# Three query steps ahead of the small inverse, the value projection copied to SBUF, and chunk, state and local products that alternate between the row halves

## Chip, cores and metric

The kernel runs on 1 core of one Trainium2 chip. The metric is the device time of one execution in microseconds (us); the times shown are medians of repeated runs. TensorE (PE) does the matmuls and transposes, VectorE (DVE), ScalarE (ACT) and GpSimd (POOL) the elementwise work, and SyncE (SP) issues most of the DMAs.

## The reference, cut to what matters

A trunk of two layers over 256 tokens of 1024 channels, all in float32:

```python
for l in range(DEPTH):                       # DEPTH = 2
    proj = x @ w_in[l]
    y_pool = multiscale_pool(proj[..., :256], pool_w[l], pool_scale[l])
    rw_in  = centred_token_shift(proj[..., 256:1216], mu_prev[l], mu_next[l])
    y_rwkv = rwkv7_bidir(rw_in, ...)          # a forward and a backward scan, 4 heads of 64
    y_attn = gqa_axial(proj[..., 1216:], ...) # 8 query heads, 2 key heads of 64, all 256 tokens
    y = concat([y_pool, y_rwkv, y_attn]) @ w_o[l]
    x = layer_norm(ALPHA * x + y)
    x = layer_norm(ALPHA * x + hier_moe(x))   # 32 experts, 2 per token
```

One step of the RWKV scan, per head, with a state of 64x64:

```python
sk    = state @ kk_t
state = state * w_t - outer(sk, kk_t * a_t) + outer(v_t, k_t)
y_t   = state @ r_t
```

The token shift is `f + mu_prev * (f[t-1] - f) + mu_next * (f[t+1] - f)`.

## The kernel before, in words

Each layer is a mixer (`mixer`, L243 to L1011), then the routing (`route_all`), then the experts (`experts`). The expert weights stream through a ring of 22 SBUF slabs of 1 MB, 192 slabs a layer, loaded by SP in the order of the program; a slab's DMA is issued when its slot is free. Slabs of the mixer (weights and work tiles) share this ring, so the first 22 expert slabs of a layer load while its mixer runs.

The scan is computed in four chunks of 64 tokens. Each of the two directions `d` has 4 heads and 4 chunks; a tile of 128 rows holds two heads on its two row halves (`hh`, `half(0)` and `half(1)`), or two chunks by the parity of their number (`par`). The steps of the mixer's own chain, in the order of the program:

- Projections, shifts, the decay's cumulative products, and the operands `ZR`, `Bt`, `Kt` (L552 to L656). `lp` (L658 to L670): products of 32-token blocks.
- `lane_steps` (L688): six DVE steps that invert 16x16 triangular blocks, called one at a time as a generator `lanes`.
- Chunk products (`chunk_prod`, L714, tile `ap`): one call makes 16 matmuls of 64 rows, contracting over one row half, into one PSUM bank, and one masked DVE product that reads it. Four calls, each `d` and `hh`, with a lane step in front of each (L733 to L740). Then `Bn`, two sets of transposes, with the last lane steps; `AT16`, `Tp` and its transposes `TA`, `TB` by DVE (L741 to L757).
- The small inverse: products `i1` to `i5` (L787 to L849) build the inverse of a 64x64 block from 16x16 and 32x32 blocks. ACT makes the eight copies of `TTf` (L820). The value shift `vf` (L797) reads the value projection from its PSUM bank `rv[1]`.
- Key products (L850): `chunk_prod` four times from `Kt`, through the generator `key_prod`. Then `xk`, `psb` and `bon`, `Kn`, and the products `gw`, which give `Gn` and `W2` (L870 to L885).
- State products `nh` and `js` (L893 to L925), one bank for each `d` and `par`; `chain` (tile `st`), and `local_out` (tile `ya`, L944), one bank and one ACT copy for each `par`. Then `yb`, the group norm and the gate.

Beside this chain runs a second one, the generator `side` (L299), whose steps are put into the program by `upto(n)` (L523): it advances `side` until its n-th `yield`. Its steps: 1 to 8 receptance and value projection (banks `rv[0]`, `rv[1]`); 9 to 16 pooling input and key/value projection (banks `pp`, `kv`), ending with the ACT copies `u`; 17 the key normalisation and rotation (`krs`, L378 to L387); 18 to 25 the query steps k = 0 to 7 (two matmuls `pq` of 128x512 each; each also takes one step of `pooling()`, on POOL; k = 3 also transposes the keys); 26 query normalisation and rotation on ACT, DVE and POOL; 27 the pooling product `pl`; 28 and 29 query transposes; 30 the router's bias; from 31 scores, softmax, transposes and value products of the attention, then the product with `w_o`.

The order of instructions on every engine is the order of the program. PSUM has two tags: `bank` (tag r, 5 banks) for the chain and `bankc` (tag c, 3 banks) for most of `side`. `rv[1]` and the two `pq` banks are of tag c. In the program before, `upto` stands so: 15, 15, 15, 16 after the four chunk products; 17 after `i1` and the value shift; 18 after `i2`; 19 ahead of `i5`; one more step after each of the four key products (to 23); `24 + d` after each `xk`; 26 to 29 in `gw`; 31 to 34 in `nh`; 36 to 42 in `js`; 44, 46, 48, 51 around `chain` and `local_out`. So query steps k = 0 and 1 stand inside the inverse, k = 2 to 5 among the key products, k = 6 and 7 behind `xk`.

Of the kernel before, what the change touches and what calls it, by code (L numbers as in the profile page):

```python
# [13 lines left out]
OP = mybir.AluOpType  # L14
# [3 lines left out]
T = 256  # L18
# [50 lines left out]
def tile_encoder(ctx: ExitStack, tc: tile.TileContext, x_tok, x_t, w_a0, w_a1, w_b0, w_b1, w_o,  # L69
# [53 lines left out]
    E, EX, EB = mixer_slabs()  # L123
# [119 lines left out]
    def mixer(l, P, x, E, EX, block, wb, resid):  # L243
# [55 lines left out]
        def side():  # L299
# [77 lines left out]
            Va = cut(E[2], 3840, [128, 2, 128])  # L377
            krs = []  # L378
            tail = [cut(E[2], 512 * n + 320, [128, 128]) for n in range(1, 6)]
            for i in range(2):  # L380
                ps = ps_kv[:, 256 * i:256 * i + 256]
                A.copy(Va[:, i], ps[:, 128:256])
                rk = rms(ps[:, 0:128], 2, "rk", tail[0])
                kr = rope(ps[:, 0:128], 2, gck, gsk, i, tail[1 + i], tail[3 + i])
                G.tensor_tensor(kr, kr, rk.rearrange("p (h d) -> p h d", d=1).to_broadcast([128, 2, 64]), op=OP.mult)
                krs.append(kr)
            yield  # L387
            rq, qrs = [], []
# [408 lines left out]
        for j in range(2):  # L797
            shift(rv[1][:, T * j:T * j + T], vf[:, j], 6 + j)
        upto(17)

        def key_prod(d):
            at = s4(4 + d).rearrange("p (h q a t) -> p h q a t", h=2, q=4, a=2)
            for hh in range(2):
                chunk_prod(Kt[d], d, hh, at)
                yield
            ATk[d] = at.rearrange("p h q a t -> p (h q) a t")

        kp = [key_prod(d) for d in range(2)]
        for d in range(2):
# [4 lines left out]
            TN.append(t_)  # L814
        upto(18)
        for d in range(2):
# [33 lines left out]
        for d in range(2):  # L850
            for _ in kp[d]:
                upto(sent[0] + 1)
            to_tok(lambda j, i: ZR[d][:, 0, j, 128 * i:128 * i + 128], "Zn", ZR[d][:, 0])
        for d in range(2):
# [4 lines left out]
            A.copy(ATb[d][:, :, 0], ps)  # L859
            upto(24 + d)  # L860
        psb = bank("psb")
# [8 lines left out]
        for d in range(2):  # L870
            w2 = s2([128, 8, 64], "W2")
            for h in range(2):
# [16 lines left out]
        for d in range(2):  # L889
            HT.append(ZR[d][:, 1].rearrange("p j (c t) -> p j c t", t=64))  # L890
            IN.append(s1([128, 2, 2, 64], "IN"))
            PJ.append(late[:, 1, d].rearrange("p (j c) t -> p j c t", j=2))
        for d in range(2):  # L893
            for par in range(2):
                nn = 1 if par else 2
                cs = [2 * i + par for i in range(2) if 2 * i + par != order[d][0]]
                p1 = bank("nh").rearrange("p (j c t) -> p j c t", j=2, t=64)
                for c in cs:
                    for jh in range(2):
                        for hh in range(2):  # L900
                            q = 4 * hh + 2 * jh + c // 2
                            mm(p1[half(hh), jh, c // 2], Gn[d][half(par), q], ATb[d][half(par), q, 1])
                            if c == nn:
                                mm(p1[half(hh), jh, 2], Gn[d][half(par), q], nat(Bn[d], q, par))
                for c in cs:
                    V.tensor_tensor(HT[d][:, :, c], HT[d][:, :, c], p1[:, :, c // 2],
                                    op=OP.subtract)
                V.tensor_tensor(IN[d][:, :, par],
                                eye64.rearrange("p (j t) -> p j t", j=1).to_broadcast([128, 2, 64]),
                                p1[:, :, 2], op=OP.subtract)  # L910
                upto(31 + 2 * d + par)
        for d in range(2):
            for par in range(2):
                js = [2 * i + par for i in range(2) if 2 * i + par != order[d][3]]
                p2 = bank("js").rearrange("p (j c t) -> p j c t", j=2, t=64)
                for c in js:
                    for jh in range(2):
                        for hh in range(2):
                            q = 4 * hh + 2 * jh + c // 2
                            acc(p2[half(hh), jh, c // 2], nat(Kn[d], q, par), nat(Vn, q, par), c == js[0] and jh == 0)  # L920
                            acc(p2[half(hh), jh, c // 2], nat(Bn[d], q, par), W2[d][half(par), q])
                for c in js:
                    V.tensor_tensor(PJ[d][:, :, c], p2[:, :, c // 2],
                                    pall[d][:, :, c:c + 1].to_broadcast([128, 2, 64]), op=OP.mult)
                upto(36 + 4 * d + 2 * par)  # L925
        St = [{order[d][1]: PJ[d][:, :, order[d][0]]} for d in range(2)]
# [16 lines left out]

        def local_out(par):  # L944
            p1 = bank("ya").rearrange("p (j i t) -> p j i t", j=2, t=64)
            for d in range(2):
                for jh in range(2):
                    for i in range(2):
                        for hh in range(2):
                            q = 4 * hh + 2 * jh + i  # L950
                            acc(p1[half(hh), jh, i], nat(Vn, q, par), ATk[d][half(par), q, 1], d == jh == i == 0)
                            acc(p1[half(hh), jh, i], W2[d][half(par), q], ATb[d][half(par), q, 1])
            A.copy(wkv.rearrange("p j (i r) t -> p j i r t", r=2)[:, :, :, par], p1[:, :, 0:2])

        chain(1)
        upto(44)
# [3 lines left out]
        upto(48)  # L960
        local_out(1)
        upto(51)
        p3 = bank("yb").rearrange("p (j c t) -> p j c t", j=2, t=64)
# [619 lines left out]
```

## Time and profile before

| | |
|---|---|
| median of 3 runs | 1303.68 us (1299.08 to 1311.31) |
| profiled execution | 1308.36 us, its span 1306.6 us |
| granted TensorE clock, mean of the span | 0.870 |
| PE busy | 999.7 us (77%), 7547 matmuls |
| PE weight loads (PEld) busy | 490.5 us (38%) |
| DVE, ACT, POOL busy | 343.0 us (26%), 238.6 us (18%), 98.0 us (7%) |
| DMA | 438.65 MB, 336 GB/s on the mean |

The layers follow each other in the span: mixer of layer 0 to about 193 us, its experts to about 650 us, mixer of layer 1 to about 841 us, its experts to the end. In rows that list instructions, `64*64 64x128 f32` behind an operation is the tile of PE that it uses (rows and columns) and the shape of the output. Matmuls of one group are joined in a row with their count; in float32 one matmul runs as two passes, and the count `x` counts passes. "idle before <-" names what ended the engine's idle time.

### The profile page before, as it was taken

The page shows a single profiled execution, that of the slowest core. Times are in us where ns is not written, and L with a number is a line of the kernel's source. Part 1 is how long each engine was busy: PE and PEld are TensorE (multiplying, and loading weights), DVE is VectorE, ACT ScalarE, POOL GpSimd, SP SyncE. Part 2 cuts the span into 40 slices and gives each one's busy share as a digit, 9 for nine tenths or more (in the row PEclk, how much of TensorE's full clock was granted, in tenths as well). Part 3 has the DMA queues.
Part 4 walks back from the last instruction along what each step waited for, and adds up shares of the span by engine and source line. Part 5 has one row for each costly group of instructions (what it writes and reads, how often), then busy time and mean ns, then how long its engine had stood idle before and what let it go on. Part 6 is the DMA issues. An engine that isn't in the chain of part 4 may idle for free. (4 is left out here: it accounts for less than half of the span.)

```text
span 1306.6 us, 17970 instructions
## 1 busy us (share of the span) xinstructions
PE 999.7 (77%) x7547; PEld 490.5 (38%) x7547; DVE 343.0 (26%) x779; ACT 238.6 (18%) x551; POOL 98.0 (7%) x140
## 2 busy tenths in 40 slices
PE   8798988950997777686697979889429978777754
PEld 7655773330441222120286557732204412222100
DVE  5835653110010000010268286521100100010103
ACT  5224512100110101010251354220001101010100
POOL 1142100000000000000111452000000000000002
PEclk9988998985999988887798999889759997888776
DMA  9302598998999999999940136899989999999994
GB/s 373 153 34 98 214 367 351 419 418 356 401 418 419 420 420 419 419 420 421 417 184 9 35 130 259 325 413 418 419 335 420 419 419 420 420 419 419 420 420 167
DMA packets 63450, 438.65 MB, mean 336 GB/s; under 512 B 7040, under 2 KB 7296, under 8 KB 11520
## 3 DMA queue, kind: packets, MB, share of 16 engines
q1 hardware_dynamic: 62784, 436.61, 81.4%
q8 instruction: 63, 1.03, 0.3%
q10 hardware_dynamic: 576, 0.79, 0.2%
q14 instruction: 27, 0.22, 0.0%
HBM read 436.32 MB, written 1.05 MB: 335 GB/s over the span
## 5 line engine op out<-in xcount | busy, mean ns | idle before, releaser
L172 PE MATMUL pg<-w,xg 128*32 128x512 f32 x1024 | 145.7, 668 | 120.4 <-ACT xg L1205 79.3
L172 PE MATMUL py<-w,hT 128*32 128x512 f32 x1024 | 146.3, 696 | 56.2 <-DMA w<-in_e_w_dram 45.1
L172 PE MATMUL pu<-w,xg 128*32 128x512 f32 x1024 | 157.5, 702 | 41.2 <-DMA w<-in_e_w_dram 40.8
L1236 DVE TENSOR_TENSOR h<-h,pu 128x512 f32<-128x512 f32 x16 | 11.0, 688 | 435.7 <-PE pu L172 226.6
L1205 ACT ACTIVATE xg<-xg,lnc 128x128 f32<-128x128 f32 x120 | 44.9, 457 | 354.0 <-PE xg L168 246.2
L172 PEld LDWEIGHTS pg<-w,xg 128*32 128x32 f32 x1024 | 25.7, 117 | 221.3 <-ACT xg L1205 82.3
L1266 DVE TENSOR_TENSOR xr<-xr,pc 128x512 f32<-128x512 f32 x56 | 38.5, 687 | 241.0 <-PE pc L172 241.0
L172 PEld LDWEIGHTS py<-w,hT 128*32 128x32 f32 x1024 | 28.5, 116 | 156.2 <-DMA w<-in_e_w_dram 87.9
L168 PEld LDWEIGHTS xg<-OH,x 128*128 128x128 f32 x256 | 64.8, 331 | 53.5 <-issue 52.0
L168 PEld LDWEIGHTS xg<-OH,xr 128*128 128x128 f32 x256 | 64.8, 331 | 53.0 <-issue 51.5
L168 PE MATMUL xg<-OH,x 128*128 128x128 f32 x256 | 75.1, 431 | 5.4 <-PEq L1278 4.1
L168 PE MATMUL xg<-OH,xr 128*128 128x128 f32 x256 | 75.2, 432 | 5.2 <-PEq L1278 3.8
L172 PE MATMUL pc<-y,OHT 128*128 128x512 f32 x128 | 73.9, 674 | 0.0
L1258 ACT COPY y<-py 128x512 f32<-128x512 f32 x32 | 18.7, 585 | 241.5 <-PE py L172 241.5
L231 POOL TENSOR_TENSOR w<-w 128x512 fp32r<-128x512 f32 (+1 forms) x20 | 25.2, 1266 | 499.4 <-ACT w L230 496.9
L172 PEld LDWEIGHTS pu<-w,xg 128*32 128x32 f32 x1024 | 23.9, 116 | 99.4 <-DMA w<-in_e_w_dram 80.3
L269 PE MATMUL wo<-w 128*128 128x512 f32 x192 | 48.7, 409 | 5.3 <-DVE x L514 2.0
L196 POOL TENSOR_TENSOR lnmv<-lnmv,eps 128x1 f32<-128x1 f32 x8 | 4.9, 613 | 537.5 <-PE pc L172 463.5
L269 PEld LDWEIGHTS wo<-w 128*128 128x128 f32 x192 | 36.6, 194 | 16.5 <-DVE x L514 2.4
L172 PEld LDWEIGHTS pc<-y,OHT 128*128 128x128 f32 x128 | 21.4, 201 | 54.9 <-issue 49.2
L230 ACT CAST w<-w 128x512 fp32r<-128x512 f32 (+1 forms) x64 | 37.3, 602 | 22.2 <-PE wo L269 13.8
L168 PE MATMUL pq<-w 128*128 128x512 f32 x64 | 35.8, 681 | 0.5 <-DVE w L283 0.5
(330 smaller groups left out, 1095.4 us busy)
## 6 DMA issues: line engine op xcount, KB each, us to landing
w<-in_e_w_dram SPq DMA_DIRECT2D x384, 1024.0 KB, 19.9
w<-in_w_b_dram SPq DMA_DIRECT2D x8, 1024.0 KB, 18.7
w<-in_w_o_dram SPq DMA_DIRECT2D x8, 1024.0 KB, 20.0
w<-in_w_a_dram SPq DMA_DIRECT2D x4, 1024.0 KB, 13.4
lnr<-in_ln_rows_dram SPq DMA_DIRECT2D x12, 256.0 KB, 12.8
w<-in_w_a_dram SPq DMA_DIRECT2D x4, 448.0 KB, 6.4
w<-in_w_a_dram SPq DMA_DIRECT2D x2, 896.0 KB, 12.4
w<-in_cols_dram SPq DMA_DIRECT2D x2, 790.0 KB, 10.4
```

What stands on the lines that cost most here:

```text
L168: PE.matmul(ps, lhsT=lhsT, rhs=rhs, start=start, stop=True, skip_group_check=True)
L172: PE.matmul(ps, lhsT=lhsT, rhs=rhs, start=start, stop=stop)
L196: G.tensor_tensor(mv[:, 3:4], mv[:, 2:3], eps[:, 4:5], op=OP.pow)
L230: A.copy(hi, src)
L231: (V, G)[LOW[m]].tensor_tensor(lo, src, hi.bitcast(F32), op=OP.subtract)
L269: PE.matmul(ps, lhsT=l_[a], rhs=r_[b], start=first and n == 0, stop=last, skip_group_check=True)
L1205: A.activation(t_[:, k], ps[:, k], AF.Identity, scale=lnc["g1"][:, m:m + 1], bias=lnc["b1"][:, m:m + 1])
L1236: V.tensor_mul(h_, h_, ps_u)
L1258: A.copy(y_, py)
L1266: V.tensor_add(o_, o_, ps)
```

## The change

In `side`, the key normalisation moves from ahead of query step 0 to ahead of query step 4; `pooling()` begins at k = 3 instead of 0, its rest and the key transposes come at k = 6 instead of k = 3. Three query steps (k = 0 to 2) are called, by `upto(19)`, ahead of `AT16`, behind the `Bn` transposes; the rest follow at `upto(20)`, `(21)`, `(22)`, `24 + d`, and the query normalisation, step 26, stands behind `xk`.

The value projection is copied by ACT from its bank `rv[1]` to SBUF (`vraw`), behind the `lp` products, and the value shift reads the copy.

`chunk_prod` makes both row halves `hh` in one call: two banks, and matmuls that alternate between them; each of its two masked products is followed by a lane step. `nh`, `js` and `local_out` open two banks, one for each `par`, and alternate their matmuls between the parities; `local_out` is now called per direction `d`, and both its ACT copies stand behind the second call. The number of matmuls and their operands is the same.

```diff
@@ side
-            krs = []
...
-            yield
             rq, qrs = [], []
...
             for k in range(8):
-                next(pool_ops, None)
+                if k == 4:
+                    krs = []
...
+                    yield
+                if k > 2:
+                    next(pool_ops, None)
                 w = wb[1](k)
                 for i in range(2):
                     acc(ps_q[i], xw(k, 128 * i, 128 * i + 128), w, k == 0)
-                if k == 3:
+                if k == 6:
+                    for _ in pool_ops:
+                        pass
                     pkt = bankc("pkt")
@@ behind the lp products
+        vraw = cut(E[1], 2560, [128, 2, T])
+        A.copy(vraw.rearrange("p j t -> p (j t)"), rv[1])
@@
-        def chunk_prod(src, d, hh, at):
-            ps = bank("ap").rearrange("p (q t) -> p q t", q=4)
+        def chunk_prod(src, d, at):
+            ps = [bank("ap").rearrange("p (q t) -> p q t", q=4) for _ in range(2)]
             for q in range(4):
                 jh, i = q // 2, q % 2
                 for par in range(2):
                     t0 = 128 * i + 64 * par
-                    mm(ps[half(par), q].rearrange("p (a t) -> p a t", a=2), src[half(hh), jh, t0:t0 + 64],
-                       ZR[d][half(hh), :, jh, t0:t0 + 64])
-            V.tensor_tensor(at[:, hh].rearrange("p q a t -> p q (a t)"), ps, mb[d], op=OP.mult)
+                    for hh in range(2):
+                        mm(ps[hh][half(par), q].rearrange("p (a t) -> p a t", a=2), src[half(hh), jh, t0:t0 + 64],
+                           ZR[d][half(hh), :, jh, t0:t0 + 64])
+            for hh in range(2):
+                V.tensor_tensor(at[:, hh].rearrange("p q a t -> p q (a t)"), ps[hh], mb[d], op=OP.mult)
+                next(lanes, None)
@@
-            for hh in range(2):
+            if d == 0:
                 next(lanes, None)
-                chunk_prod(Bt[d], d, hh, at)
-                upto(15 + (d + hh) // 2)
+            chunk_prod(Bt[d], d, at)
+            upto(15 + d)
@@ behind the Bn transposes
-            next(lanes, None)
+        upto(19)
+        for _ in lanes:
+            pass
@@ the inverse
-            shift(rv[1][:, T * j:T * j + T], vf[:, j], 6 + j)
-        upto(17)
+            shift(vraw[:, j], vf[:, j], 6 + j)
+        upto(20)
...
-        upto(18)
+        upto(21)
...
-        upto(19)
+        upto(22)
...
-            for _ in kp[d]:
-                upto(sent[0] + 1)
+            key_prod(d)
+            upto(24 + d)
...
-            upto(24 + d)
+        upto(26)
...
-                upto(26 + 2 * d + h)
+                upto(27 + 2 * d + h)
@@ nh; js and its upto(36 + 4 * d + 2 * par), now upto(38 + 4 * d), are changed in the same way
+            p1 = [bank("nh").rearrange("p (j c t) -> p j c t", j=2, t=64) for _ in range(2)]
+            for n in range(2):
+                for jh in range(2):
+                    for hh in range(2):
+                        for par in range(2):
+                            if n < len(cs[par]):
+                                c = cs[par][n]
+                                q = 4 * hh + 2 * jh + c // 2
+                                mm(p1[par][half(hh), jh, c // 2], Gn[d][half(par), q], ATb[d][half(par), q, 1])
...
-                upto(31 + 2 * d + par)
+            upto(32 + 2 * d)
@@
-        def local_out(par):
-            p1 = bank("ya").rearrange("p (j i t) -> p j i t", j=2, t=64)
...
+        def local_out(d):
+            for jh in range(2):
+                for i in range(2):
+                    for hh in range(2):
+                        q = 4 * hh + 2 * jh + i
+                        for m in range(2):
+                            for par in range(2):
+                                acc(pya[par][half(hh), jh, i], W2[d][half(par), q] if m else nat(Vn, q, par),
+                                    (ATb if m else ATk)[d][half(par), q, 1], d == jh == i == m == 0)
+        pya = [bank("ya").rearrange("p (j i t) -> p j i t", j=2, t=64) for _ in range(2)]
...
         local_out(1)
+        for par in range(2):
+            A.copy(wkv.rearrange("p j (i r) t -> p j i r t", r=2)[:, :, :, par], pya[par][:, :, 0:2])
```

## Rows read from the trace of the kernel before

**Rows 1.** Stretches of the span; the first line names the columns, PEclk is the granted clock.
```profile
core 0: us, PE busy (x) PEld busy (x) DVE busy (x) ACT busy (x) POOL busy (x), PEclk, DMA share, GB/s
58.85:64.90 6.05, 0.00 (x0) 0.00 (x0) 5.79 (x9) 1.03 (x3) 0.00 (x0) 0.79 0.48 173
62.33:72.57 10.24, 6.48 (x193) 5.90 (x194) 6.38 (x13) 0.63 (x3) 0.00 (x0) 0.50 0.01 2
64.90:83.72 18.82, 15.85 (x460) 10.93 (x460) 8.56 (x23) 5.96 (x19) 8.59 (x13) 0.71 0.01 3
104.27:118.16 13.89, 10.65 (x99) 8.26 (x99) 6.97 (x18) 6.01 (x16) 4.04 (x5) 0.71 0.55 217
118.16:150.40 32.24, 29.95 (x467) 20.69 (x467) 24.07 (x67) 19.22 (x53) 10.31 (x8) 0.97 0.16 55
193.20:199.70 6.50, 5.89 (x32) 4.67 (x35) 1.71 (x6) 1.50 (x4) 0.00 (x0) 0.74 0.08 30
199.70:323.80 124.10, 72.17 (x469) 30.57 (x461) 18.25 (x44) 11.54 (x25) 0.00 (x0) 0.81 0.98 406
713.00:731.60 18.60, 15.85 (x460) 11.11 (x460) 8.61 (x24) 5.97 (x19) 8.35 (x12) 0.69 0.01 3
752.20:763.30 11.10, 7.41 (x100) 5.93 (x100) 6.98 (x18) 5.93 (x16) 4.06 (x5) 1.00 0.70 275
763.30:796.70 33.40, 29.43 (x467) 20.43 (x465) 27.66 (x67) 19.22 (x53) 20.15 (x16) 1.00 0.13 38
840.80:847.90 7.10, 6.49 (x36) 5.09 (x39) 1.96 (x9) 1.51 (x5) 0.00 (x0) 0.76 0.15 56
```

**Rows 2.** DVE in order of time, 55 to 65 us: start us, us, instruction.
```profile
55.09 0.69 DVE L722 TENSOR_TENSOR w<-ap,kc 128x512 f32<-128x512 f32 x1 [0.90 <-PE ap L172]
...
63.81 1.04 DVE L754 STREAM_TRANSPOSE TA<-Tp 128x512 f32<-128x512 f32 x1
```

**Rows 3.** PE in order of time, 51 to 57 us, the chunk products.
```profile
51.00 1.09 PE L172 MATMUL ap<-w,sga 64*64 64x128 f32 x16
...
53.95 2.09 PE L172 MATMUL ap<-w,sga 64*64 64x128 f32 x48
```

**Rows 4.** PE in order of time, 64 to 88 us, inverse and key products.
```profile
64.91 1.92 PE L172 MATMUL i<-TA,AT 64*64 64x32 f32 x32 [6.07 <-DVE TA L754]
...
76.45 0.85 PE L174 MATMUL i<-TN,w 32*32 32x32 f32 x48
...
78.76 0.44 PE L174 MATMUL i<-TN,w 32*32 32x32 f32 x16 [1.45 <-issue]
79.13 3.56 PE L168 MATMUL pq<-w 128*128 128x512 f32 x4
...
84.75 1.98 PE L168 MATMUL pq<-w 128*128 128x512 f32 x4
86.66 1.09 PE L172 MATMUL ap<-w,sga 64*64 64x128 f32 x16
```

**Rows 5.** ACT in order of time, 57 to 80 us.
```profile
57.14 0.65 ACT L329 COPY w<-pp 128x256 f32<-128x256 f32 x2 [11.85 <-PE pp L168]
...
72.31 0.26 ACT L382 COPY w<-kv 128x128 f32<-128x128 f32 x1
...
75.48 3.00 ACT L820 COPY late<-i 32x256 f32<-32x256 f32 x8
78.50 0.58 ACT L730 COPY Vn<-tk 128x512 f32<-128x512 f32 x1
```

**Rows 6.** PE in order of time, 103 to 120 us, the pooling product.
```profile
109.18 0.65 PE L172 MATMUL pl<-w 64*64 64x256 f32 x4 [2.51 <-DVE w L360]
```

**Rows 7.** Groups of PE, 668 to 800 us: passes | busy us, mean ns | idle.
```profile
L168 PE MATMUL ya<-w,Vn 64*64 64x64 f32 x64 | 4.0, 222 | 0.0
...
L168 PE MATMUL js<-Vn,Kn 64*64 64x64 f32 x48 | 3.4, 230 | 0.0
...
L172 PE MATMUL nh<-w,late 64*64 64x64 f32 x48 | 3.0, 230 | 0.0
```

**Rows 8.** PE in order of time, 44 to 50 us, the lp products.
```profile
44.04 0.76 PE L174 MATMUL lp<-sga,w 64*32 64x32 f32 x64
```

More of the change, by code (lines that the diff above doesn't have):

```diff
@@ L377, in side @@
             Va = cut(E[2], 3840, [128, 2, 128])
-            krs = []
[L379 to L386, printed above, removed]
-            yield
             rq, qrs = [], []
@@ L398, in side @@
             for k in range(8):
-                next(pool_ops, None)
+                if k == 4:
+                    krs = []
+                    tail = [cut(E[2], 512 * n + 320, [128, 128]) for n in range(1, 6)]
+                    for i in range(2):
+                        ps = ps_kv[:, 256 * i:256 * i + 256]
+                        A.copy(Va[:, i], ps[:, 128:256])
+                        rk = rms(ps[:, 0:128], 2, "rk", tail[0])
+                        kr = rope(ps[:, 0:128], 2, gck, gsk, i, tail[1 + i], tail[3 + i])
+                        G.tensor_tensor(kr, kr, rk.rearrange("p (h d) -> p h d", d=1).to_broadcast([128, 2, 64]), op=OP.mult)
+                        krs.append(kr)
+                    yield
+                if k > 2:
+                    next(pool_ops, None)
                 w = wb[1](k)
@@ L797, in mixer @@
         for j in range(2):
-            shift(rv[1][:, T * j:T * j + T], vf[:, j], 6 + j)
-        upto(17)
+            shift(vraw[:, j], vf[:, j], 6 + j)
+        upto(20)
         def key_prod(d):
             at = s4(4 + d).rearrange("p (h q a t) -> p h q a t", h=2, q=4, a=2)
-            for hh in range(2):
-                chunk_prod(Kt[d], d, hh, at)
-                yield
+            chunk_prod(Kt[d], d, at)
             ATk[d] = at.rearrange("p h q a t -> p (h q) a t")
-        kp = [key_prod(d) for d in range(2)]
         for d in range(2):
@@ L893, in mixer @@
         for d in range(2):
-            for par in range(2):
[L895 to L906, printed above, removed]
+            p1 = [bank("nh").rearrange("p (j c t) -> p j c t", j=2, t=64) for _ in range(2)]
+            cs = [[2 * i + par for i in range(2) if 2 * i + par != order[d][0]] for par in range(2)]
+            for n in range(2):
[6 more added lines that the diff above has]
+                                mm(p1[par][half(hh), jh, c // 2], Gn[d][half(par), q], ATb[d][half(par), q, 1])
+                                if c == (1 if par else 2):
+                                    mm(p1[par][half(hh), jh, 2], Gn[d][half(par), q], nat(Bn[d], q, par))
+            for par in range(2):
+                for c in cs[par]:
+                    V.tensor_tensor(HT[d][:, :, c], HT[d][:, :, c], p1[par][:, :, c // 2],
                                     op=OP.subtract)
@@ L909, in mixer @@
                                 eye64.rearrange("p (j t) -> p j t", j=1).to_broadcast([128, 2, 64]),
-                                p1[:, :, 2], op=OP.subtract)
-                upto(31 + 2 * d + par)
+                                p1[par][:, :, 2], op=OP.subtract)
+            upto(32 + 2 * d)
         for d in range(2):
-            for par in range(2):
[L914 to L923, printed above, removed]
+            p2 = [bank("js").rearrange("p (j c t) -> p j c t", j=2, t=64) for _ in range(2)]
+            js = [[2 * i + par for i in range(2) if 2 * i + par != order[d][3]] for par in range(2)]
+            for n in range(2):
+                for jh in range(2):
+                    for hh in range(2):
+                        for m in range(2):
+                            for par in range(2):
+                                if n < len(js[par]):
+                                    c = js[par][n]
+                                    q = 4 * hh + 2 * jh + c // 2
+                                    acc(p2[par][half(hh), jh, c // 2], nat((Kn, Bn)[m][d], q, par),
+                                        W2[d][half(par), q] if m else nat(Vn, q, par), n == jh == m == 0)
+            for par in range(2):
+                for c in js[par]:
+                    V.tensor_tensor(PJ[d][:, :, c], p2[par][:, :, c // 2],
                                     pall[d][:, :, c:c + 1].to_broadcast([128, 2, 64]), op=OP.mult)
-                upto(36 + 4 * d + 2 * par)
+            upto(38 + 4 * d)
         St = [{order[d][1]: PJ[d][:, :, order[d][0]]} for d in range(2)]
@@ L942, in mixer @@
         wkv = s2([128, 2, 4, 64], "wkv")
-        def local_out(par):
-            p1 = bank("ya").rearrange("p (j i t) -> p j i t", j=2, t=64)
[L946 to L953, printed above, removed]
+        def local_out(d):
+            for jh in range(2):
+                for i in range(2):
+                    for hh in range(2):
+                        q = 4 * hh + 2 * jh + i
+                        for m in range(2):
+                            for par in range(2):
+                                acc(pya[par][half(hh), jh, i], W2[d][half(par), q] if m else nat(Vn, q, par),
+                                    (ATb if m else ATk)[d][half(par), q, 1], d == jh == i == m == 0)
+        pya = [bank("ya").rearrange("p (j i t) -> p j i t", j=2, t=64) for _ in range(2)]
         chain(1)
@@ L961, in mixer @@
         local_out(1)
+        for par in range(2):
+            A.copy(wkv.rearrange("p j (i r) t -> p j i r t", r=2)[:, :, :, par], pya[par][:, :, 0:2])
         upto(51)
```

## The prediction

> **What bounds the kernel now.** I read the stretches of the span first (busy time, granted clock and DMA share in each), then the order of time on PE, VectorE (DVE) and ScalarE (ACT) inside a mixer. In the expert stages DMA is the bound: from 199.7 to 323.8 us its share is 0.98 at 406 GB/s while PE is busy 72 of 124 us [rows 1]. In the mixers it is not: shares of 0.01 to 0.16, PE nearly always busy [rows 1]. Just before each expert stage DMA is idle for 6.50 and 7.10 us (share 0.08 and 0.15) [rows 1]: all 22 ring slots are full, and the stream goes on only when the experts free the first slot. So whatever a mixer saves before that point moves the whole rest of the program forward, one for one, once per layer.
>
> Inside a mixer the reader is to see three things. PE stands still for 6.05 us while DVE computes the small inverse: its first inverse product waits 6.07 us for the transpose of Tp, which ends at 64.85 us [rows 1, 2, 4]. The granted clock then falls to 0.50 (1.2 GHz) and stays there from 62.33 to 72.57 us, with the small inverse products that follow [rows 1]. And matmuls of 64 rows run only two at a time: 16 passes of a chunk product take 1.09 us, but 48 passes in a row, of groups on both row halves, take 2.09 us [rows 3].
>
> All sums below are made against the profiled execution: 1308.36 us, of which 1306.6 is the span and 1.8 lies around it. The median of the three runs, 1303.68, is 4.68 lower; I take that off at the end.
>
> **The change part by part,** in us saved per layer.
>
> *Three query steps ahead.* A query step is two matmuls of 128x512 (4 passes); from the start of one to that of the product behind it is 86.66 - 84.75 = 1.91 [rows 4]. Three are 5.73, and they now stand in the hole. The four chunk products there take 1.02 + 2.02 today; as two alternating pairs they should take 2 x 1.02, so PE comes to the hole 1.0 earlier, at 57.85, and is done at 63.6. DVE's chain in front of the transpose of Tp loses one wait, 0.90 for a chunk product of the second row half [rows 2]; I take 0.85. The first inverse product then starts at 64.05, with PE idle 0.5 instead of 6.07. Saved: 5.73 of steps that need no time later, and 0.85. Both ends: if nothing goes ahead, 0; more than the hole, 6.05 + 0.85, cannot be had here.
>
> *Value projection copied out.* The query steps need PSUM banks that the value projection holds until its token shift, which now comes after the steps. One copy of 128x512 on ACT per layer is added; a like one (Vn) took 0.58 [rows 5]. It falls where ACT is idle for 11.85 [rows 5]; cost 0, and 0.6 if that cover were gone. Behind it on ACT wait the copies u, at 57.14, 6 us later. The shift reads SBUF instead of PSUM: 0, with a tenth either way. The moved key normalisation, pooling and key transposes add no instruction and no DMA; POOL keeps their order, and no SP wait changes place.
>
> *The inverse, first product to first key product:* 18.82 and 18.60 [rows 1]. It holds two query steps before and after. At the low clock one of them takes 3.56 instead of 1.98 [rows 4], the earlier one is about 1.0 late, and the two first products take 1.92 each [rows 4], about half of that at full clock: 4.5 lost to the clock. Against it stands a new order on ACT: the key normalisation (72.31 to 75.48, DVE in between) moves from before the second inverse product to after it, in front of the eight copies of TTf, 3.00 us [rows 5]. Counted from the first inverse product these end at 13.6 today; by the same durations they end at 12.8 afterwards, so the stretch can't be shorter than about 13.9. Ends: 4.9 saved if the clock stays up, 0 if it falls all the same: some 4 us of small products still follow one another. Their clock row [rows 1] shows that such work did not raise it. I take 2.8.
>
> *Key products.* Four groups of 1.03 (83.72 to 84.75 [rows 4]) become two: 1.8 saved after switching. Ends: 0 (no overlap) and 2.06.
>
> *The stretch from W2/G products to the first scores,* 13.89 and 11.10 [rows 1]. The query normalisation (step 26) now starts before psb and the Kn transposes instead of after the first of these products. The pooling product waits 2.51 for it today [rows 6]; with 2.7 us more of PE work in between I leave 1.0. But bon and W2 queue on DVE behind the query rotation, and PE's third product group behind bon's bank: half a microsecond goes back. Saved 0.9 in layer 1. In layer 0 the same work ran at a clock of 0.71 against 1.00 [rows 1], worth 2.8; I count 2.0 of it, so 2.9. Ends: 2 us lost (bon and W2 wait for the whole rotation) and 4.5 saved in layer 0, 2 in layer 1.
>
> *nh, js and ya products.* 80, 96 and 128 passes (48 + 32, 48 + 48 and 64 + 64, two interleaved groups each, of which one row stands) busy for 3.0, 3.4 and 4.0 [rows 7], some 31 to 37 ns a pass with two in flight; four in flight would halve them, 5.2 off PE. PE isn't alone there: DVE is busy 24.07 of 32.24, in layer 1 27.66 of 33.40 [rows 1], and the attention steps wait for it. I take 2.2 and 1.2; ends 0 and 5.2. The two ACT copies of wkv, now behind the last product, lie beside the yb products: 0.
>
> One rule speaks against this term. The Trainium skill, "TensorE: Matmul & The Clock Gate", section "Wait — 56ns, not 53.3ns?", says that matmuls never start closer than about 25 ns, however few their columns. Here 64 passes in four row and column strips took 0.76 us, 12 ns each [rows 8], so the row does not bear it out; by the rule the three products would keep 25 ns a pass (saving 2.8 on PE instead of 5.2), and the sum would be some 1.7 us higher.
>
> Sum: layer 0 5.73 + 0.85 + 2.8 + 1.8 + 2.9 + 2.2 = 16.3; layer 1 5.73 + 0.85 + 2.8 + 1.8 + 0.9 + 1.2 = 13.3; together 29.6. 1308.36 - 29.6 = 1278.8, and less 4.7: **1274 us**. The case's own range: with the better end of the inverse and 4.5/2.0 and 4.0/2.5 for the last two stretches 39.6 saved, 1264; with these three at zero 16.8 saved, 1287.
>
> **The rivals.**
> - *Alternation gives nothing*: two in flight stay two, because the second row half's passes queue. The key, nh, js and ya terms and some 0.6 of the first go: 2 x 1.8 + 3.4 + 1.2 = 8.2, 1282. For it: one group alone never has more than two passes in flight. Against it: the 48 passes, 2.09 us instead of 3 x 1.02 [rows 3].
> - *The waits only move*: the inverse stays at the low clock and behind the ACT copies, and bon and W2 eat what the pooling product gains: 2 x 2.8 + 3.8 = 9.4 less, 1283. For it: the two chains on ACT and DVE are as long as before [rows 5]. Against it: the 6 us hole in front of the drop is gone.
> - *DMA hides it*: the first 22 slabs come no earlier, so that only the idle 6.50 + 7.10 [rows 1] can be won: 1290. Against it: the slots of these slabs are freed by the mixer itself and move with it.
> - *The steps do not run ahead*, held by a bank: 11.5 and the clock's 5.6 go, 1291. Against it: both banks are released before the hole.
> - *Slower than before*: PE outruns its instruction supply. It stood 1.45 us in the middle of a product without waiting for anything that the profile shows, after 48 passes in 0.85 us [rows 4]. Ten product groups per layer (4 chunk, 2 each of nh, js, ya) would be issued twice as fast; if each stood 2 us, 40 us are lost: 1314. It decides from 29.6 / 20 = 1.5 us a group. Against it: the 48 overlapping passes ran without a hole [rows 3].
>
> **How the numbers follow.** Forecast 0.60; alternation without effect 0.13; waits that only move 0.15; DMA 0.05; steps not ahead 0.03; slower 0.04. The forecast's range with the next two lies between 1264 and 1287; for the unknown ends on both sides I give 1262 to 1291, which leaves out the slower case, half of the DMA and bank cases, and a tail below. About 1% (13 us) is what a measurement of this kernel can tell from no change. Faster by more than that (under 1290.6): nearly all of the first three and half of the DMA case, 0.89. Slower (over 1316.7): 0.02. Within: 0.09.
>
> **What would show it.** Right, if in the profile after: twelve pq passes stand behind the Bn transposes and the wait of the first inverse product is under 1.5 us; the chunk product groups show 32 passes in about 1.1 us and ya 64 in about 1.1; no stretch of clock 0.50 begins at the inverse, or one of 3.4 us; the key products begin about 15 to 16.5 us after the first inverse product; DMA still pauses some 6 us before each expert stage, about 16 and 30 us earlier than now. Wrong, if the passes per group stay at 55 and 31 ns (alternation), if a new wait of over 2 us stands before i5, gw or ptp (waits move), if the pause before the experts is gone (DMA), or if PE shows gaps by "issue" in the product groups (instruction supply).

## The result, and the profile after

The changed kernel takes 1287.75 us, median of 4 runs (1285.02 to 1289.5), against 1304.68 us (1299.08 to 1311.31) in the same runs of the kernel before: ratio 0.9854, 95% interval 0.9824 to 0.9884. It is 16.9 us faster; 29.6 had been forecast, to 1274. The profiled execution has a span of 1283.1 us, 23.5 under that of before.

The stretches of the span after, the eight that answer to [rows 1] (window, length, busy time of each engine with its instructions, granted clock, DMA share, GB/s):

```profile
core 0: us, PE busy (x) PEld busy (x) DVE busy (x) ACT busy (x) POOL busy (x), PEclk, DMA share, GB/s
65.49:84.60 19.11, 15.63 (x460) 10.21 (x461) 8.70 (x23) 5.09 (x16) 6.83 (x10) 0.73 0.16 57
698.07:719.71 21.64, 16.05 (x461) 10.54 (x461) 8.69 (x23) 5.07 (x16) 6.44 (x9) 0.76 0.15 51
97.25:106.95 9.70, 7.88 (x123) 5.96 (x122) 7.07 (x19) 5.66 (x15) 4.06 (x5) 1.00 0.54 210
732.35:742.06 9.71, 7.89 (x124) 5.97 (x123) 7.08 (x19) 5.66 (x15) 4.06 (x5) 1.00 0.57 212
106.95:135.06 28.11, 24.31 (x445) 16.36 (x444) 22.94 (x67) 18.85 (x53) 10.31 (x8) 1.00 0.19 63
742.06:773.70 31.64, 25.75 (x445) 17.64 (x444) 25.05 (x67) 18.95 (x53) 20.20 (x16) 0.95 0.11 37
179.91:186.77 6.86, 6.86 (x36) 4.52 (x40) 2.39 (x13) 2.87 (x11) 0.00 (x0) 0.57 0.01 1
821.00:825.78 4.78, 4.78 (x30) 2.75 (x33) 1.95 (x11) 2.40 (x11) 0.00 (x0) 0.67 0.00 0
```

Each line has its fellow in [rows 1]. Two of the mixer's parts became shorter here: the gw stretch from 13.89 and 11.10 to 9.7, the one behind it from 32.24 and 33.40 to 28.1 and 31.6. DMA still pauses ahead of the experts (last two lines), so the mixer's gain passes on. The inverse, first product to first key product, did not become shorter: 18.82 and 18.60 before, 19.11 and 21.64 after.

PE in order of time after, chunk products to first inverse product of layer 0 (before: [rows 3, 4]):

```profile
52.69 1.10 PE L172 MATMUL ap<-w,sga 64*64 64x128 f32 x32
...
55.65 1.10 PE L172 MATMUL ap<-w,sga 64*64 64x128 f32 x32
...
59.39 5.32 PE L168 MATMUL pq<-w 128*128 128x512 f32 x12
65.49 1.12 PE L172 MATMUL i<-TA,AT 64*64 64x32 f32 x32 [0.79 <-DVE TA L765]
```

32 chunk passes (16 matmuls of two passes each, made by one `chunk_prod`; before, one made 8) take the time of 16, the twelve query passes fill the hole, and the first inverse product waits 0.79 us instead of 6.07 and takes 1.12 instead of 1.92. So far all is as forecast. The same engine, layer 1, inside the inverse:

```profile
701.57 3.51 PE L168 MATMUL pq<-w 128*128 128x512 f32 x4
705.01 0.75 PE L174 MATMUL i<-IX,TB 32*32 32x32 f32 x64
...
706.28 0.58 PE L174 MATMUL i<-TB,IX 32*32 32x32 f32 x46
711.00 0.29 PE L174 MATMUL i<-TB,IX 32*32 32x32 f32 x13 [4.13 <-issue]
...
714.48 0.79 PE L174 MATMUL i<-TN,w 32*32 32x32 f32 x21 [0.24 <-issue]
715.20 3.52 PE L168 MATMUL pq<-w 128*128 128x512 f32 x4
```

PE stands 4.13 us in the middle of i3, for nothing that its row names (in layer 0 1.49, and 0.78 in i4), and both query steps run at the low clock. Before, the only such stop was in i4, 1.45 us in layer 0 [rows 4] and 1.28 in layer 1. SP's queue after shows what is new beside it:

```profile
705.11 0.33 SPq L1042 DMA_DIRECT2D w<-in_e_w_dram  x1
```

Query step 3 was the last reader of the first half of its weights. Their slab is free when that step ends, now ahead of i2, and SP issues an expert slab of 1 MB into it. What DMA moves while PE stands, in two windows of the changed kernel, 705.00 to 708.50 us and 708.50 to 711.00 us:

```profile
q1 hardware_dynamic: 96, 0.79, 67.9%
...
q1 hardware_dynamic: 48, 0.26, 26.5%
q8 instruction: 1, 0.02, 2.2%
```

(Queue, packets, MB, share of 16 engines.) A packet of the instruction queue comes only in the second window, at 708.61, when most of the slab has passed, and PE goes on 2.4 us after it. That PE lacks instructions is read from this order: in all stops of over 0.2 us in the inverse, in the fourteen traces of this case, PE goes on 2.2 to 2.8 us after a packet of that queue has begun (once 3.4).

In layer 0 the slab is issued ahead of i2 as well, and yet the stop is short:

```profile
71.81 0.33 SPq L1042 DMA_DIRECT2D w<-in_e_w_dram  x1
75.37 0.36 PE L174 MATMUL i<-TB,IX 32*32 32x32 f32 x21 [1.49 <-issue]
```

There the instruction packet began at 72.77, together with the slab's first packet (72.76); in layer 1 it began 2.5 us behind it.

Groups of PE by line and shape after, layer 1, which answer to [rows 7]:

```profile
L172 PE MATMUL ap<-w,sga 64*64 64x128 f32 x128 | 4.4, 275 | 0.0
...
L168 PE MATMUL ya<-w,Vn 64*64 64x64 f32 x64 | 2.2, 226 | 0.0
...
L172 PE MATMUL nh<-w,late 64*64 64x64 f32 x48 | 2.0, 232 | 0.0
```

ya went from 4.0 to 2.2 us, nh from 3.0 to 2.0, and ap, four groups of 32, from 7.5 to 4.4. js gained less here, 3.4 to 2.7; in layer 0, at full clock, it takes 2.2.

### The profile page after: what moved, and what is told of

The parts are those of the page before. It is cut to its first block, busy times and chain, and to the rows that moved or that the text cites. A ratio compares the mean times of both kernels' runs of the same rounds, so it can differ in the third digit from the quotient of the medians.

```text
span 1283.1 us, 17982 instructions
## 1 busy us (share of the span) xinstructions
PE 989.3 (77%) x7547; PEld 478.2 (37%) x7547; DVE 339.4 (26%) x779; ACT 238.8 (19%) x553; POOL 98.2 (8%) x140
## 3 DMA queue, kind: packets, MB, share of 16 engines
HBM read 436.32 MB, written 1.05 MB: 341 GB/s over the span
## 5 line engine op out<-in xcount | busy, mean ns | idle before, releaser
L172 PE MATMUL pg<-w,xg 128*32 128x512 f32 x1024 | 152.2, 695 | 119.9 <-ACT xg L1221 78.8
L172 PE MATMUL pu<-w,xg 128*32 128x512 f32 x1024 | 158.2, 705 | 36.5 <-DMA w<-in_e_w_dram 36.4
L172 PEld LDWEIGHTS py<-w,hT 128*32 128x32 f32 x1024 | 29.6, 118 | 153.9 <-DMA w<-in_e_w_dram 79.7
L230 ACT CAST w<-w 128x512 fp32r<-128x512 f32 (+1 forms) x64 | 37.3, 602 | 22.4 <-PE wo L269 14.0
## 6 DMA issues: line engine op xcount, KB each, us to landing
w<-in_w_b_dram SPq DMA_DIRECT2D x8, 1024.0 KB, 18.7
```

What stands on the lines that cost most here:

```text
L172: PE.matmul(ps, lhsT=lhsT, rhs=rhs, start=start, stop=stop)
L230: A.copy(hi, src)
```

## The experiments

Times are medians of six runs (twelve for the copy of the kernel before), each beside runs of the kernel before on the same chip, whose medians lay between 1304.6 and 1306.5. The two medians of the changed kernel lie 2.1 us apart, so small differences are read from stretches of the traces.

**The kernels again.** No edit. First the kernel before.

> The kernel before, a second time, to see which of its stretches repeat. Theory (the low clock in the stretch from psb to the first scores of layer 0, 10.2 us long, was chance, and the sum counted it as a gain although the median holds it only in part): that stretch comes out near 12.9 us in both layers instead of 15.72 and 12.90; PE's wait of 1.3 to 1.5 us in i4 and the 6.07 us hole repeat; the stretch from the first inverse product to the first key product stays between 16.5 and 19. Rival (the 15.72 us belong to layer 0): 15.5 to 16 again in layer 0.

Median 1308.14 (1298.22 to 1318.38; ratio to the other copies 1.001, 0.9978 to 1.0041). The profiled run has a span of 1296.6, ten less than that of the same program before. psb to first scores (the gw stretch of [rows 1] with psb and the Kn transposes), in both layers, first of the first execution, then of this second one:

```profile
102.45:118.16 15.71, 12.47 (x109) 9.38 (x108) 7.66 (x19) 6.34 (x16) 4.04 (x5) 0.74 0.55 201
750.39:763.29 12.90, 9.21 (x110) 7.05 (x109) 7.67 (x19) 6.25 (x16) 4.06 (x5) 1.00 0.65 244
```

```profile
100.31:113.49 13.18, 10.67 (x109) 8.16 (x108) 7.67 (x19) 6.37 (x16) 4.06 (x5) 0.87 0.62 239
741.95:755.17 13.22, 10.71 (x110) 8.20 (x109) 7.67 (x19) 6.37 (x16) 4.06 (x5) 0.87 0.64 239
```

So the 15.7 us of layer 0 did not repeat, as the theory has it: the clock was lower there in the first execution (0.74 for 0.87). The hole (6.05, 6.06) and the stop in i4 (0.83, 1.05, a little shorter) repeat; the inverse took 16.57 and 16.82.

> The changed kernel itself, a second time, to see what of its trace repeats. Theory (the stall in the small products is made by the slab's transfer and by fast passes in a row): PE's wait in i2 and i3 by nothing that the profile shows is again 3.5 to 5 us in layer 1 and 1 to 2.5 in layer 0; the low clock falls at other places, so that a stretch without a change moves by up to 4 us; median 1286 to 1290. Rival (the 4.13 us were chance): the wait in layer 1 comes out under 2.5.

Median 1289.84, 14.8 us under the kernel before beside it (ratio 0.9871, 0.9829 to 0.9913). The stop in i3 of layer 1 is 3.67 us, 1.85 in layer 0: it belongs to the kernel. The inverse took 17.09 and 23.24.

**The slab later.**

```diff
-            for k in range(8):
+            for k, kw in enumerate((0, 1, 2, 4, 5, 3, 6, 7)):
-                w = wb[1](k)
+                w = wb[1](kw)
-                    acc(ps_q[i], xw(k, 128 * i, 128 * i + 128), w, k == 0)
+                    acc(ps_q[i], xw(kw, 128 * i, 128 * i + 128), w, k == 0)
```

> The changed kernel, with the query steps taking the eight weight blocks in the order 0, 1, 2, 4, 5, 3, 6, 7, so that the first weight slab is freed among the key products and not ahead of the small products i2 and i3; nothing else differs. Theory (the 1 MB expert slab that SP now issues at 71.81 and 705.11 us runs across the fetch of PE's instructions): the stall in i2 and i3 of layer 1 falls from 4.13 us to about 1.5, that of layer 0 stays near 1.5, the stretch from the first inverse product to the first key product goes from 21.6 to about 19.0 us in layer 1 and stays at 19.1 in layer 0; the time is about 2.6 us under the changed kernel's 1287.75. Rival (256 fast passes in a row outrun the supply whatever else DMA does): 4.13 and 21.6 us stay, and so does the time.

Median 1288.59. PE in this version, layer 1, i2 to i4:

```profile
706.36 0.75 PE L174 MATMUL i<-IX,TB 32*32 32x32 f32 x64
...
710.09 0.30 PE L174 MATMUL i<-TB,IX 32*32 32x32 f32 x13 [1.94 <-issue]
...
713.58 0.79 PE L174 MATMUL i<-TN,w 32*32 32x32 f32 x21 [1.27 <-issue]
```

With the slab gone the stop comes after the same passes but lasts 1.94 instead of 4.13. In the DMA queues of this version, from 706.30 to 708.80 us, nothing but the instruction packet is there:

```profile
q8 instruction: 1, 0.02, 2.9%
```

So about 2 us are the transfer's in layer 1 (4.13 and 3.67 in the changed kernel's two executions), and about 1.9 are there without it. In layer 0 nothing was gained: its stops are 2.11 and 1.59 with the slab gone, longer than the 1.5 expected and than the changed kernel's 1.49 and 0.78; there the packet had not come behind the slab. The stretch went to 20.25, not 19.0: a second stop of 1.27, where the changed kernel has 0.24, came in i4. The time is a miss: no gain, though the stretch became shorter; the low clock took some of it back among the key products (12.34 us there in layer 1, 10.72 in layer 0).

**A query step between i2 and i3.**

```diff
-                if k == 4:
+                if k == 5:
                     krs = []
-        upto(20)
+        upto(19)
...
-        upto(21)
+        upto(20)
...
-        upto(22)
+        upto(21)
```

> The changed kernel, with query step 3 between i2 and i3 instead of behind i1, step 4 ahead of i5, and the key normalisation, which has no PE work, behind i5 instead of between i2 and i3. Theory (a stall comes after some 170 fast passes in a row): no stall in i2 or i3; one of about 1.5 us in i4, as in the kernel before, and longer in layer 1 if the slab's transfer falls on it; stretch from the first inverse product to the first key product about 17.5 us in layer 0 and 17.5 to 20 in layer 1, so 1.5 to 5 us under the changed kernel. Rival (the clock alone sets this stretch, and it falls whenever the small products come): 19 us in both layers, time as the changed kernel's.

Median 1286.8, 1.0 to 3.0 under the changed kernel's two medians. The inverse takes 16.16 us in layer 0, with one stop of 0.91, better than expected, and 20.65 in layer 1. PE there:

```profile
706.15 0.81 PE L174 MATMUL i<-TN,w 32*32 32x32 f32 x45
710.56 0.63 PE L174 MATMUL i<-TN,w 32*32 32x32 f32 x19 [3.60 <-issue]
```

No stop in i2 or i3; in layer 1 the slab, issued at 704.42, now falls on i4. Both edits together:

> The changed kernel with query step 3 between i2 and i3, step 4 ahead of i5 and the key normalisation behind i5, and also the weight blocks in the order 0, 1, 2, 4, 5, 3, 6, 7, so that the slab's transfer comes among the key products. Theory: the 3.6 us stall that the step between i2 and i3 alone left in layer 1, beside the slab's transfer, goes to 0.9 as in layer 0; stretch from the first inverse product to the first key product about 16 to 17 us in both layers, the time 3 to 5 us under the version with the step between alone (1286.8), 1282 to 1284. Rival (the stall there isn't the slab's): 20 us in layer 1 and 1287.

Median 1282.91, as expected, 6.9 under the changed kernel on the same chip; the inverse took 16.11 and 15.04 us, its stops in i4 1.32 and 1.16 (and 0.22 in i3 of layer 0):

```profile
707.12 0.50 PE L174 MATMUL i<-TN,w 32*32 32x32 f32 x19 [1.16 <-issue]
```

So both parts are shown by edits: the stop in i3 goes with the step between, and what the slab adds in layer 1 with its own edit (3.60 to 1.16). A stop of 1.2 to 1.3 us in i4 stays with both edits.

**TB in a place of its own.**

```diff
-        TB = s2([128, 16, 2, 16], "TB")
+        TB = cut(E[1], 0, [128, 16, 2, 16])
```

> The changed kernel with TB in SBUF space of its own, so that its transpose on DVE needn't wait until the first i1 group has read AT16. Theory (the holes in front of the small products cost PE time): TB ends 1.2 us earlier, the hole of 1.2 us between the two i1 groups goes, the stretch from the first inverse product to the first key product is 1.1 us shorter in both layers, the time 2 us under the changed kernel's. Rival (PE's supply of instructions sets this stretch): the stall in i2 and i3 grows by what the hole gave, stretch and time stay.

Median 1285.51. The hole between the i1 groups is gone. In layer 0 the rival holds: the stop grew to 3.65 (1.49 and 1.85 in the changed kernel) and the stretch is 19.21 (19.11 and 17.09). In layer 1 it doesn't: the stop is 4.13 (4.13 and 3.67) and the stretch became shorter, 20.67 (21.64 and 23.24), as the theory has it. The time is 4.3 under the changed kernel on the same chip, more than the expected 2; that stays unexplained, as the profiled execution, the slowest of the six, has the span of the changed kernel's (1285.3). With the other two edits:

> The version with step 3 between i2 and i3 and the later slab, with TB in space of its own as well. Theory (the parts add): stretch from the first inverse product to the first key product about 15 us in both layers, time 1280 to 1282. Rival (supply of instructions or the clock take back what the hole gave): as without TB's place, 1283 or more.

Median 1277.93, ratio to before 0.9776 (0.9733 to 0.9819), better than expected; the inverse took 13.25 and 14.50. PE in layer 1:

```profile
694.32 1.12 PE L172 MATMUL i<-TA,AT 64*64 64x32 f32 x32 [1.03 <-DVE TA L765]
695.32 1.12 PE L172 MATMUL i<-w,AT 64*64 64x32 f32 x32
...
703.80 0.56 PE L174 MATMUL i<-TN,w 32*32 32x32 f32 x19 [1.06 <-issue]
```

By the medians TB's place is worth 5.0 us here and was worth 4.3 in the changed kernel, so it pays with the long stop and without it. The inverse is 2.9 and 0.5 shorter than without it, in layer 0 at a higher clock as well (1.00 for 0.89); where the rest comes from isn't shown.

**Four steps ahead,** TB in its place, plain order of the weights.

```diff
-                if k == 4:
+                if k == 6:
                     krs = []
...
-                if k == 6:
+                if k == 7:
                     for _ in pool_ops:
...
-        upto(19)
+        upto(20)
...
-        upto(20)
```

> The changed kernel with four query steps ahead of the inverse (the slab is freed there, in DVE's time), step 4 between i2 and i3, step 5 ahead of i5, the key normalisation ahead of step 6 and the key transposes behind step 7, TB in space of its own, weight blocks in their plain order. Theory (the fourth step costs 0.9 us of wait for the first inverse product and gives 1.9 among the key products, and the slab's transfer lies in the hole): first chunk product to first inverse product about 14.0 us, stretch from there to the first key product 13 to 14.5, from the first key product to psb 9.6; 1 us a layer under the version with three steps and the later slab (1277.93), 1274 to 1278. Rival (the transfer falls on the instruction fetch of i1 or i2, or the key transposes come too late): a stall over 2.5 us, or a wait for the keys ahead of the first scores, and 1280 or more.

Median 1275.92, ratio 0.9767 (0.9737 to 0.9798): the best version, with the one before it within their spread. First chunk to first inverse product 13.86 and 13.66, key products to psb 9.00 in both layers. The inverse is a miss, 15.6 instead of 13 to 14.5: two stops, of 1.0 and 1.6 us, in either layer. In layer 1, where the slab was issued at 693.90, ahead of i1's second group:

```profile
700.65 0.34 PE L174 MATMUL i<-w,IX 32*32 32x32 f32 x18 [1.01 <-issue]
...
704.42 0.57 PE L174 MATMUL i<-TN,w 32*32 32x32 f32 x24 [1.58 <-issue]
```

The first stop comes only 45 passes behind a query step, so it isn't the length of a run of fast passes alone that brings one. The traces speak for the slab's transfer, moved ahead of it: the instruction packet began at 698.26, just as that transfer ended, 4.5 us behind the first inverse product (4.4 in layer 0), and in the version above, without a slab there and without a stop in i3, only 3.4 us behind it. Moving the slab away in this version was not tried.

**The alternation,** off in the changed kernel and alone in the kernel before. The edit of the first, for the chunk products (nh, js and ya in the same way, `par` outermost):

```diff
-            for q in range(4):
-                jh, i = q // 2, q % 2
-                for par in range(2):
-                    t0 = 128 * i + 64 * par
-                    for hh in range(2):
+            for hh in range(2):
+                for q in range(4):
+                    jh, i = q // 2, q % 2
+                    for par in range(2):
+                        t0 = 128 * i + 64 * par
```

> The changed kernel with all its banks, steps and waits, but the matmuls of the chunk, key, nh, js and ya products in the order one row half (or one parity) after the other. Theory (alternation halves these groups): the two key product groups take 2.0 us each instead of 1.1, 1.9 more a layer; ya 1.9 instead of 1.0 twice a layer, nh and js about 0.5 more each, of which the stretch from the first scores to the output projection shows 2 to 4 in layer 0 and 1 to 2 in layer 1; together 6 to 9 us over the changed kernel, 1294 to 1297. Rival (alternation gives nothing that counts): within 2 us of the changed kernel.

Median 1292.01, 2 to 4 us over the changed kernel: less than expected, more than the rival's 2 by little. Key products to psb 11.69 in layer 1 (10.72 with it; 15.04 in layer 0, at a clock of 0.77), first scores to gate product 38.34 and 42.77 (36.48 and 40.01). The profiled execution is the slowest of the six. With the chunk and key products alone undone:

> The changed kernel with the chunk and key products in the order one row half after the other; nh, js and ya alternate. Theory (alternation halves a group's own time, and only the two key groups stand on the path): 0.5 us more for each of 4 key groups, the stretch from the first key product to psb 11.7 us instead of 10.7, and some 2 us over the changed kernel in the time; the first inverse product no more than 0.4 us later. Rival (the chunk groups ahead of the hole count as well): 4 us or more.

Median 1289.65, 1.9 over one and 0.2 under the other median of the changed kernel; that stretch 11.69 in both layers, as expected, 1 us a layer. With nh, js and ya alone undone:

> The changed kernel with the nh, js and ya products in the order one parity after the other; chunk and key products alternate. Theory (PE's time in these groups is on the path): the stretch from the first scores to the gate product 38.3 us instead of 36.5 in layer 0 and about 42 instead of 40 in layer 1, the time 3 to 5 us over the changed kernel. Rival (DVE and ACT set that stretch, PE has room): within 1.5 us of the changed kernel.

Median 1296.39, 6.5 to 8.6 over the changed kernel, above what was expected and above the version with everything undone, so it holds some of the medians' spread. The stretches from the first scores to the gate product, first of this version, then of the changed kernel:

```profile
108.13:146.47 38.34, 34.97 (x488) 24.84 (x485) 26.54 (x72) 21.68 (x58) 10.28 (x8) 1.00 0.36 132
745.89:788.37 42.48, 37.97 (x488) 26.79 (x485) 29.20 (x72) 21.78 (x58) 20.16 (x16) 0.92 0.29 114
```

```profile
106.95:143.43 36.48, 32.68 (x488) 22.32 (x485) 26.73 (x73) 21.51 (x58) 10.31 (x8) 1.00 0.37 141
742.06:782.07 40.01, 34.12 (x487) 23.60 (x484) 28.84 (x73) 21.60 (x58) 20.20 (x16) 0.96 0.29 112
```

At equal clock, in layer 0, PE is busy 2.29 us less and the stretch is 1.86 shorter: PE's time there is on the path.

Alone in the kernel before (the changed kernel with `side`, the value shift and every `upto` put back):

```diff
-        vraw = cut(E[1], 2560, [128, 2, T])
...
-        upto(19)
...
-        upto(20)
+        upto(17)
...
-            upto(24 + d)
+            upto(21 + 2 * d)
```

> The kernel before with the alternating products alone: the query steps, the key normalisation and the value shift stand where they stood. Theory (the parts add): the hole of 6 us stays and is 1 us longer, key products 2 us less a layer, the rest 1 to 4 us less a layer, together 6 to 9 us under the kernel before, 1296 to 1299. Rival (most of the changed kernel's gain is the alternation, and the steps ahead only fill a hole and then wait): 12 us or more under the kernel before.

Median 1295.25, ratio to before 0.9921 (0.989 to 0.9952): 11 us, more than the theory's 6 to 9 and a little less than the rival's 12. Key products to psb 16.31 (18.72 before). The hole is 5.79 and 6.16, not 1 us longer, since DVE's chain became shorter by as much. The parts don't add: 11.2 alone and 14.5 for the steps without it make 25.7, and both together gave 16.9 and 14.8. Where the rest goes isn't settled; both versions with the steps have the long stop in layer 1 (5.21 without the alternation), which the alternation alone has not (1.37).

## Why the prediction was right, and by how much it missed

Stretches between the first matmuls of groups, in us, mean of the two executions of each kernel; forecast and measured gain, layer 0 / layer 1:

| stretch | before | after | forecast | measured |
|---|---|---|---|---|
| start to chunk products | 50.1 / 44.9 | 52.0 / 44.9 | 0 | -1.9 / 0.0 |
| to first inverse product | 13.9 / 13.9 | 13.2 / 13.0 | 0.85 | 0.7 / 0.9 |
| inverse, to key products | 17.7 / 17.7 | 18.1 / 22.4 | 2.8 | -0.4 / -4.7 |
| to psb | 18.7 / 18.7 | 10.7 / 10.7 | 7.5 | 8.0 / 8.0 |
| to first scores | 14.5 / 13.1 | 11.6 / 11.6 | 2.9 / 0.9 | 2.8 / 1.4 |
| to gate product | 39.6 / 41.8 | 36.5 / 40.1 | 2.2 / 1.2 | 3.1 / 1.7 |
| to the experts | 39.6 / 40.4 | 40.8 / 41.6 | 0 | -1.2 / -1.2 |

Together 11.2 and 6.1, 17.3, near the 16.9 and 14.8 of the medians; forecast were 29.6. The time lies inside the stated range by its width more than by its working: the inverse came out below the lower end given for it, and the other terms of the sum, none of them at its lower end, made up for that.

- *Three steps ahead, key products:* right. PE fills the hole, 0.79 us of wait remain, the stretch to psb lost 8.0 (5.73 + 1.8 forecast). The pooling product waits 0.65 us [rows 6: 2.51], where 1.0 had been left.
- *The gw stretch:* right in layer 1. In layer 0 2.5 of its 15.72 us belonged to that execution; against the second one the gain is 1.55, not 2.9, so some two thirds of the 2.0 counted there for the clock were not the change's to win.
- *Value projection:* free, as said, so far as layer 1 shows it (0.0 ahead of the chunk products); no run takes the copy out alone. In layer 0 the low clock fell on the stretch ahead of the chunk products in both executions after, and not in the two before; the version with the alternation alone has it too, without that copy, and two versions with the copy don't. What brings it isn't settled.
- *nh, js, ya:* right. The 3.1 of layer 0 holds a lower clock of the first execution before (40.61 us at 0.97); from the second (38.57 at 1.00) to 36.48 it is 2.1, for 2.2 forecast; in layer 1 1.7 for 1.2. PE itself gained less than thought: at full clock the three rows of [rows 7] went from 10.4 (layer 1 before) to 6.4 us (layer 0 after), 4.0 for 5.2, and a larger part of that stood on the path. The rule of the Trainium skill ("TensorE: Matmul & The Clock Gate", "Wait — 56ns, not 53.3ns?") of 25 ns from start to start is not borne out: 64 passes of one ya group, interleaved with 64 of the other, were busy 2.2 us, some 17 ns a pass; the measurement decides.
- *The inverse:* this step failed, and with it most of the miss: 10.7 of 12.3 us. It was forecast at 2.8 saved a layer, between 0 and 4.9; it lost 0.4 and 4.7. The clock did stay up through i1, as forecast. Two sentences were wrong. "No SP wait changes place": query step 3 frees a slab, and SP's issue moved with it from the key products (737.63 us before) to the front of i2. And the instruction supply was looked for in the wrong place: the rival had seen the 1.45 us stop [rows 4], but priced it for the alternating groups, which show none. It grew in the small products: the key normalisation, a step without PE work, was put between i2 and i3, so that 256 fast passes follow each other and PE, it seems, has used up its instructions before the next packet is there, and in layer 1 the slab's transfer came on top. With both undone (step between, slab later) the inverse took 16.11 and 15.04, 1.6 and 2.7 under the kernel before: the 2.8 had been there to win.
- *The clock:* it still falls in the inverse of the changed kernel (its means 0.73 and 0.76 above, 0.80 and 0.63 in the second execution). It was also lower behind the gate product, 0.90 and 0.88 in layer 0 for 0.92 before, 0.89 and 0.85 in layer 1 for 0.89 and 0.92; the 1.2 us a layer of the last row go with that. The forecast counted 2.0 us of clock in the gw stretch of layer 0 and also took off the 4.68 by which the profiled execution stood over the median; part of that was probably the same low clock, counted twice.
- *DMA hides it, steps held by a bank, alternation without effect:* none came. From a layer's first expert matmul to the next layer or the end the profiled executions took 456.3 and 459.8 us, before 455.9 and 460.2; the chunk and ya groups run nearly twice as fast, nh and js by less, and the twelve query passes stand where they should.

## What to carry to other kernels

When a step is moved, list what its last read sets free: a buffer that is reused by a DMA moves that DMA as well, and here a 1 MB transfer that started ahead of an instruction packet made PE stand about 2 us longer in a run of very short instructions. A slow matmul group between groups of fast ones took the stop in i3 away. Look at two executions before a stretch's clock is priced as a gain.

## What had not been expected of the hardware

PE seems to run out of instructions in passes of 32x32, which start every 8 to 9 ns at full clock (64 in 0.75 us). It stood once or twice in the inverse of every execution. In layer 1 the longest stop was 1.05 to 1.94 us in six executions without a slab's transfer near it, and 3.6 to 5.2 in seven where the slab's first packet was 2.3 to 3.5 us ahead of the instruction packet. In layer 0 it was 0.8 to 2.1 without the slab, 3.1 to 3.7 where the slab was 1.5 to 2.0 us ahead of the packet, and 0.9 to 2.7 where the packet came first or with it: so it seems to count which of the two began first. The places belong to the program: counted from the first of the inverse's 460 passes, the stops of the changed kernel come after pass 236 or 363 in layer 0 and after 244 or 371 in layer 1, in both executions and in all five versions that keep its order of query steps, with the slab or without, and two stops in one inverse lie 127 passes apart in every trace that has two. So 127 passes seem to come with each packet; whether PE stands at the end of them, and how long, would then be a matter of when the next one began. And one program's spans differ by 10 us (1306.6 and 1296.6), nearly all of it in the mixers (9.8 us), mostly where the granted clock was lower (0.91 and 0.93 over the two mixers for 0.94 and 0.94).
